# Layer 0's gated mixer: the gate product over all features for each chunk of K, with part of the conditioning on VectorE

## The chip, the cores and the metric

The kernel runs on one core of a Trainium2 chip. The core has five engines that work side by side, each through its own queue in order: TensorE (PE, with its weight loads shown as PEld), VectorE (DVE), ScalarE (ACT), GpSimd (POOL) and SyncE (SP), which here only issues transfers. Transfers run on 16 DMA engines. Matmuls write to PSUM, which has eight banks of 2 KB in each of 128 partitions. The metric is the device time of one execution in microseconds (us); several executions are timed and the median is given. One execution is also recorded by the hardware profiler; its times are counted from the start of the recorded span.

## The reference

A trunk of four layers over 256 tokens of width 1024, in float32. Each layer has a token mixer and a gated feed-forward part (FFN), and both are steered by a conditioning vector c. Layers 0 and 3 use a gated MLP as mixer. What matters here:

```python
c_act = jax.nn.silu(c)
mod = c_act @ ada_w[i] + ada_b[i]
sh1, sc1, g1, sh2, sc2, g2 = jnp.split(mod, 6, axis=-1)
h = modulate(rmsnorm(x, mix_norm_g[i]), sh1, sc1)
...
z = jax.nn.gelu(h @ w_in)
u, v = jnp.split(z, 2, axis=-1)
v = layernorm(v, ln_g, ln_b)
n = S // GM_CHUNK
v = v.reshape(B, n, GM_CHUNK, GM_GROUPS, GM_GROUP_DIM)
mask = jnp.tril(jnp.ones((GM_CHUNK, GM_CHUNK), dtype=bool))
ws = jnp.where(mask[None], w_s, jnp.zeros_like(w_s))
sv = jnp.einsum('gts,bnsgd->bntgd', ws, v) + b_s.T[None, None, :, :, None]
y = u * sv.reshape(B, S, GM_INNER)
return y @ w_out
```

`u` and `v` have 2048 features each. `mod` has 6 x 1024 values for each layer; the first 2048 (shift and scale) are needed before the first product of layer 0.

## The kernel before

The program is written with a framework that takes the instructions in program order, schedules them on the engines by priority and data, and sets the semaphores. The order in which the engines run them can therefore differ from the source; `tc.issue_after` forces an order on one engine.

**Products in three parts.** Weights come as 1 MB units of 128 x 2048 (`raw`, five buffers). `conv_half` splits a half unit into a rounded part `wh` (a cast on ACT, line 207) and the rest `wl` (a subtraction on VectorE, line 208), five buffers each. The activations are split in the same way into `hh` and `hlo`. `mm3` (lines 238 to 240) forms each product from three matmuls. `unit` hands out the next unit, and starts the loads and conversions of those after it.

**Conditioning.** `mod` of the layers is made in two ways. `ada_tensor` multiplies on TensorE (line 293). `ada_vector` multiplies rows of the weights with the spread vector `cbc` and sums them on VectorE (line 315), 1024 columns at a time, two for a 1 MB load. `pacing`, called once for each unit, starts such loads at the rates of `RATE` (a share of a load for each unit, for both kinds), and runs each two units later. In the last units of a stage it starts none (`left`). `need` runs what is still missing when its value is due.

**The first product.** For layer 0, `ada_first` (line 336) makes shift and scale for one chunk of 128 features at a time: a 1 MB load `adaf`, 64 small matmuls for each; `first_store` turns the result into columns (line 343), and `modulate_chunk` makes `nt`, `hh` and `hlo` of the chunk (lines 443 to 445). The order is written out by hand in `FIRST`: `a` is such a chunk of conditioning, `v` a chunk of the product, `d` the load of a unit, `p` the loads of late parameters and of the spread vector. The product `v` is computed token by feature, with K chunks of 128 inside. Its blocks 0 and 1 (1024 features, four banks) run along with the conditioning, chunk by chunk, from units that hold two K chunks each (`proj_tok_first`). Blocks 2 and 3 follow from units of 512 features (`proj_tok`).

**Behind it.** `gmlp` takes Gelu and sums of each block of `v` (line 561), squares around a provisional mean (line 575), the mean and root (lines 605 to 616). The layer-norm gain `Gb` and the bias `bs` come as one row and are spread by GpSimd (lines 584 and 592). `wsp`, the masked spatial weights times the inverse deviation, is made on VectorE (line 619), `v` is shifted and scaled in place (line 623), and `rsum`, the row sums of the spatial weights, come from TensorE (line 598). Then eight units of `u`: 48 products in `proj_pair`, four spatial matmuls `sv` (line 638), and the gating on VectorE and ACT (lines 632 to 646). The output product `go` (eight units) reads the gated `y` over 16 K chunks and updates `x`.

**PSUM.** The banks are four of tag `acc`, three of tag `misc` and one for `adaps`.

Of the kernel before, what the change touches and what calls it, by code (L numbers as in the profile page):

```python
# [8 lines left out]
F32 = mybir.dt.float32  # L9
# [29 lines left out]
FIRST = "a0 d v0 a1 a2 d v1 a3 v2 a4 d v3 a5 v4 a6 d v5 a7 v6 p v7"  # L39
# [10 lines left out]
RATE = {("mix", 0): (0.05, 0.4), ("u", 0): (0.1, 0.9), ("go", 0): (0.35, 0.7), ("up", 0): (0.05, 0.05),  # L50
# [41 lines left out]
def build(ctx, tc, A, out, stages=None):  # L92
# [34 lines left out]
    nc.scalar.dma_start(cin[:], A["c"])  # L127
    n0, n1 = _COLS["ada_b"] + 48, _COLS["lb"]
# [3 lines left out]
    ident = one.tile([P, P], F32, name="ident")  # L132
# [3 lines left out]
    def late_consts():  # L136
        with tc.issue_after(state["lastdma"]):
            nc.sync.dma_start(prm[:, n1:], A["prm"][:, n1:])
            nc.sync.dma_start(ident[:], A["ident"])
# [130 lines left out]
    adaps = pp.tile([P, 2, 256], F32, tag="ada", name="adaps", bufs=1)  # L270
# [6 lines left out]
    def ada_tensor(l, u):  # L277


        def load(i):  # L280
# [3 lines left out]
            def run():  # L284
                h = ADA_P.index((l, u)) % 2
                ps = adaps[:, h, :]
# [39 lines left out]
    def ada_first(l, c):  # L326

        raw = wp.tile([P, KC, 4, 64], F32, tag="raw", name=f"adaf{c}", bufs=NRAW)
        nc.sync.dma_start(raw[:].rearrange("p a b c -> p (a b c)"), A["ada0"][l, c])
        ps = misc(f"adaf{c}", (P, 64))  # L330
        with contextlib.ExitStack() as es:
            if "pe" in firsts:
                es.enter_context(tc.issue_after(firsts["pe"]))
            for kc in range(KC):
                for j in range(4):
                    i = pe.matmul(ps[32 * j : 32 * j + 32, :], crep(kc), raw[:, kc, j, :], start=kc == 0, stop=kc == KC - 1,
                                  tile_position=(0, 32 * j))
            firsts["pe"] = getattr(i, "ins", i)
        firsts[c] = ps

    def first_store(l, c):
        tr = t1(f"adaft{c}", 64)
        dve.transpose(tr[:], firsts[c][:])
        for e in range(2):
            b = 8 * e + c
            dve.tensor_tensor(mod[:, l, b : b + 1], tr[:, 32 * e : 32 * e + 1], prm[:, col("ada_b", l * 48 + b) : col("ada_b", l * 48 + b) + 1],
                              op=ALU.add)
        mod_post(l, 8 + c, 1)
# [158 lines left out]
    def proj_tok(blocks, name, sink, b0=0):  # L507

        for b in range(b0, blocks):
# [10 lines left out]
            for t in range(2):  # L520
                sink(b, t, ps[t])

    def proj_tok_first(name, sink, start=None):

        ps = [acc(f"{name}{i}") for i in range(4)]

        def chunk(kc):
            if kc % 2 == 0:
                firsts["w"] = unit(1, 0) if start else unit(2)
            with contextlib.ExitStack() as es:  # L530
                if start and kc < KC - 1:
                    es.enter_context(tc.issue_after(firsts["pe"]))
                for b in range(2):
                    a, bl = hl(firsts["w"], (kc % 2) * 1024 + b * 512, 512)
                    for t in range(2):
                        mm3(ps[2 * b + t][:], hh[:, kc, t * P : t * P + P], hlo[:, kc, t * P : t * P + P], a, bl, kc == 0, kc == KC - 1)
            firsts["pe"] = state["mm"]

        if start:
            start(chunk)  # L540
        else:
            for kc in range(KC):
                chunk(kc)
        for i in range(4):
            sink(i // 2, i % 2, ps[i])
# [10 lines left out]
    def gmlp(l, j, start=None):  # L556
        v = [big(f"v{t}") for t in range(2)]
        sums = sm("vsum", 8)

        def sink(b, t, ps):  # L560
            i = act.activation(v[t][:, 512 * b : 512 * b + 512], ps[:], AF.Gelu_apprx_tanh, accum_out=sums[:, 4 * t + b : 4 * t + b + 1])
            state["gelu"] = getattr(i, "ins", i)

        proj_tok_first("v", sink, start)
        if start:
            pace("mix", l, 20)
        proj_tok(3, "v", sink, 2)

        nsh = sm("nsh", 2)
# [8 lines left out]
        dve.tensor_reduce(nsh[:], sums[:].rearrange("p (t q) -> p t q", t=2)[:, :, 0:3], axis=AX.X, op=ALU.add)  # L578
        dve.tensor_scalar_mul(nsh[:], nsh[:], -4.0 / (3 * GI))
        for q in range(3):  # L580
            squares(q)
        Gb = big("Gb")
        nc.scalar.dma_start(Gb[0:1, :], A["gmg"][j : j + 1])
        pool.partition_broadcast(Gb[:], Gb[0:1, :])
        wr = big("ws", (P, 2, 8, P))
        ws = wr[:, 0]
        rsum = wr[:, 1]
        nc.scalar.dma_start(ws, A["gmws"][j])
        bs = big("bs", (P, 8, P))
        bsf = bs[:].rearrange("p g t -> p (g t)")  # L590
        nc.scalar.dma_start(bsf[0:1, :], A["gmbs"][j : j + 1])
        pool.partition_broadcast(bsf, bsf[0:1, :])
        proj_tok(4, "v", sink, 3)
        pool.affine_select(ws, ws, pattern=[[0, 8], [1, P]], compare_op=ALU.is_ge, fill=0.0, base=0,
                           channel_multiplier=-1)
        for h in range(2):
            ps = misc("rsum")
            pe.matmul(ps[:], onesw[:], wr[:, 0, 4 * h : 4 * h + 4, :].rearrange("p g t -> p (g t)"), start=True, stop=True)
            act.copy(rsum[:, 4 * h : 4 * h + 4, :].rearrange("p g t -> p (g t)"), ps[:])
# [17 lines left out]
        for g in (slice(0, 2), slice(2, 8)):  # L617
            for t in range(2):
                dve.tensor_scalar_mul(wsp[:, t, g], ws[:, g], rs[:, t : t + 1])
# [5 lines left out]
        pace("u", l)  # L625
        for i in range(8):
            ps = proj_pair(hk, lk, KC, f"u{i}")
            if i == 0:
                state["chain"] = tuple(getattr(s, "ins", s) for j, s in enumerate((warm, rec, root)) if GCH >> j & 1)
# [16 lines left out]
            split(yh(2 * i, 2), yl(2 * i, 2), u[:])  # L646
        pace("go", l)
# [248 lines left out]
    def hgrn(l):  # L896
# [51 lines left out]
        def isink(b, t, ps):  # L948
            act.copy(iv[:, t, 512 * b : 512 * b + 512], ps[:])
# [197 lines left out]
    if not quick:  # L1147
        nc.sync.dma_start(prm[:, n0:n1], A["prm"][:, n0:n1])
        nc.sync.dma_start(cbc[:], A["cb"])
        act.activation(cbc[:], cbc[:], AF.Silu)  # L1150
# [18 lines left out]
    for kind, l in stages:  # L1169
# [3 lines left out]
        if kind == "mix":  # L1173
# [3 lines left out]
            if l % 3 == 0:  # L1177
                if quick:
                    quick = False
                    ada_first(l, 0)  # L1180
                    bc0 = rms_bc(cur["st"], D, "n0")

                    def start(chunk):
                        for step in FIRST.split():
                            if step == "d":
                                dma_next()
                                continue
                            if step == "p":
                                with tc.issue_after(state["lastdma"]):
                                    nc.sync.dma_start(prm[:, n0:n1], A["prm"][:, n0:n1])  # L1190
                                conv_load(l)
                                late_c()
                                continue
                            c = int(step[1])
                            if step[0] == "a":
                                if c:
                                    ada_first(l, c)
                                first_store(l, c)
# [116 lines left out]
```

## Time and profile before

| | us |
|---|---|
| median of the three runs (1376.57 to 1381.03) | 1377.04 |
| the profiled execution | 1377.02 |
| its span | 1375.2 |
| start of the first v product, in the span | 11.84 |
| start of the first u product | 70.86 |
| end of the last u unit's sv, about | 124.4 |

The granted TensorE clock of the profiled execution is 0.998 of full speed. To read the tables: "busy" is the time in which an engine executes, and "idle before, releaser" the time in which it stood still ahead of an instruction, with the one that let it go. A row of the timeline has its start, its length, engine, source line, operation, output and inputs. Lengths of matmuls overlap, since they are pipelined: the distance of two starts is what one costs.

### The profile page before, as it was taken

How to read it: one execution, taken by the hardware profiler on the slowest of the kernel's cores; microseconds unless marked ns; L12 is line 12 of the kernel's file. 1: busy time of each engine (PE TensorE's matmuls, PEld its weight loads, DVE VectorE, ACT ScalarE, POOL GpSimd, SP SyncE). 2: the span in 40 equal slices, each digit the busy share in tenths (PEclk: the TensorE clock that was granted, in tenths of full speed). 3: DMA queues.
4: the chain of work that ended last, by engine and by line, in shares of the span. 5: the costliest groups of instructions: out<-in, count | busy, mean ns of one | idle time of the engine just before them, and what ended most of it. 6: DMA issues, size and time to landing. Idle time of an engine off the chain costs nothing.

```text
span 1375.2 us, 29290 instructions
## 1 busy us (share of the span) xinstructions
PE 1348.0 (98%) x12372; PEld 1283.2 (93%) x12372; DVE 1088.5 (79%) x1760; ACT 770.8 (56%) x1202; POOL 17.6 (1%) x19
## 2 busy tenths in 40 slices
PE   8999999999999999999999999999999999999997
PEld 6799999999998899999987889999987999999997
DVE  5699798889786798897789889889674863888843
ACT  3765366664466566654666546666356553666633
POOL 0100000000000000000010000000001000000000
PEclk9999999999999999999999999999999999999999
DMA  9869955557866366688576677558646464455531
GB/s 384 333 247 338 392 188 204 195 215 316 364 227 265 132 237 245 233 325 363 183 276 217 266 280 279 213 183 352 219 148 244 167 228 171 154 184 184 184 123 31
DMA packets 49483, 326.23 MB, mean 237 GB/s; under 512 B 5956, under 2 KB 9028, under 8 KB 11974
## 3 DMA queue, kind: packets, MB, share of 16 engines
q1 hardware_dynamic: 47568, 322.72, 62.2%
q8 instruction: 97, 1.59, 0.5%
q10 hardware_dynamic: 1784, 1.65, 0.3%
q14 instruction: 34, 0.28, 0.1%
HBM read 323.29 MB, written 1.05 MB: 236 GB/s over the span
## 4 chain that ended last, share of the span: by engine, by line
PE 92%; DMA 2%; DVE 2%; ACT 2%; issue 1%; DVEq 0%; SPq 0%; ACTq 0%
PE up L238 12%; PE up L239 12%; PE up L240 12%; PE dn L238 5%; PE dn L239 4%; PE dn L240 4%; PE go L238 2%; PE go L239 2%; PE go L240 2%; PE u L239 2%; PE u L238 2%; PE u L240 2%; PE adaps L293 2%; PE v L238 2%; PE v L239 2%; PE v L240 2%
## 5 line engine op out<-in xcount | busy, mean ns | idle before, releaser
L207 ACT CAST wh<-raw 128x1024 fp32r<-128x1024 f32 x426 | 434.8, 1031 | 387.8 <-PE up L239 170.0
L208 DVE TENSOR_TENSOR wl<-raw,wh 128x1024 fp32r<-128x1024 f32 x426 | 511.7, 1207 | 159.9 <-ACT wh L207 158.5
L238 PE MATMUL up<-hh,wh 128*128 128x256 f32 x1408 | 397.7, 283 | 2.6 <-ACT hh L444 2.5
L240 PE MATMUL up<-hh,wl 128*128 128x256 f32 x1408 | 397.6, 283 | 0.0
L239 PE MATMUL up<-hlo,wh 128*128 128x256 f32 x1408 | 397.4, 283 | 0.1
L238 PEld LDWEIGHTS up<-hh,wh 128*128 128x128 f32 x1408 | 269.7, 192 | 5.3 <-ACT hh L444 4.5
L239 PEld LDWEIGHTS up<-hlo,wh 128*128 128x128 f32 x1408 | 269.8, 192 | 0.6 <-DVE hlo L445 0.5
L240 PEld LDWEIGHTS up<-hh,wl 128*128 128x128 f32 x1408 | 270.1, 192 | 0.0
L238 PE MATMUL dn<-gh,wh 128*128 128x256 f32 x528 | 149.9, 284 | 1.5 <-ACT y L1094 1.5
L239 PE MATMUL dn<-gl,wh 128*128 128x256 f32 x528 | 149.4, 283 | 0.0
L240 PE MATMUL dn<-gh,wl 128*128 128x256 f32 x528 | 149.4, 283 | 0.0
L315 DVE CUSTOM_DVE_ANT_0 adaw<-adaw,cbc,prm 128x1024 f32<-128x1024 f32 x104 | 131.2, 1275 | 0.0
L1094 ACT ACTIVATE y<-up,cwb 128x256 f32<-128x256 f32 x176 | 98.6, 560 | 10.0 <-DVE y L1096 9.9
L238 PEld LDWEIGHTS dn<-gh,wh 128*128 128x128 f32 x528 | 101.3, 192 | 2.0 <-ACT y L1094 1.7
L239 PEld LDWEIGHTS dn<-gl,wh 128*128 128x128 f32 x528 | 101.3, 192 | 0.0
L240 PEld LDWEIGHTS dn<-gh,wl 128*128 128x128 f32 x528 | 101.3, 192 | 0.0
L1096 DVE SCALAR_TENSOR_TENSOR y<-up,cwb,y 128x254 f32<-128x254 f32 x176 | 84.5, 480 | 4.7
L1095 DVE SCALAR_TENSOR_TENSOR y<-up,cwb,y 128x255 f32<-128x255 f32 x176 | 83.9, 477 | 0.9 <-ACT y L1094 0.8
L238 PE MATMUL u<-hh,wh 128*128 128x256 f32 x256 | 74.0, 289 | 0.0
L238 PE MATMUL go<-yh,wh 128*128 128x256 f32 x256 | 73.3, 287 | 0.0
L240 PE MATMUL u<-hh,wl 128*128 128x256 f32 x256 | 72.4, 283 | 0.0
L239 PE MATMUL u<-hlo,wh 128*128 128x256 f32 x256 | 72.4, 283 | 0.0
(340 smaller groups left out, 2470.7 us busy)
## 6 DMA issues: line engine op xcount, KB each, us to landing
raw<-up SPq DMA_DIRECT2D x88, 1024.0 KB, 4.8
adaw<-adad SPq DMA_DIRECT2D x52, 1024.0 KB, 7.9
adaw<-adap SPq DMA_DIRECT2D x36, 1024.0 KB, 7.6
raw<-dn SPq DMA_DIRECT2D x32, 1024.0 KB, 4.8
raw<-gmu SPq DMA_DIRECT2D x16, 1024.0 KB, 4.8
raw<-gmo SPq DMA_DIRECT2D x16, 1024.0 KB, 4.8
raw<-gmv SPq DMA_DIRECT2D x15, 1024.0 KB, 6.2
raw<-dn SPq DMA_DIRECT2D x16, 768.0 KB, 5.4
```

Of the source, the lines that this page charges most:

```text
L207: act.copy(wh[:, :w], raw[:, o : o + w])
L208: i = dve.tensor_tensor(wl[:, :w], raw[:, o : o + w], wh[:, :w].bitcast(F32), op=ALU.subtract)
L238: pe.matmul(ps, lh, rh, start=start, stop=False)
L239: pe.matmul(ps, lh, rl, start=False, stop=False)
L240: i = pe.matmul(ps, ll, rh, start=False, stop=stop)
L293: pe.matmul(ps[32 * j : 32 * j + 32, :], crep(kc), raw[:, k, j, :], start=kc == 0, stop=kc == KC - 1, tile_position=(0, 32 * j))
L315: dve.tensor_tensor_reduce(raw[:, e, :], raw[:, e, :], cbc[:], 1.0, prm[:, c0 : c0 + 1], ALU.mult, ALU.add, mod[:, l, b : b + 1])
L1094: act.activation(y[:], ps[:, e, :], AF.Identity, bias=b, scale=w[2])
L1095: dve.scalar_tensor_tensor(y[:, 1:], ps[:, e, : S - 1], w[1], y[:, 1:], op0=ALU.mult, op1=ALU.add)
L1096: dve.scalar_tensor_tensor(y[:, 2:], ps[:, e, : S - 2], w[0], y[:, 2:], op0=ALU.mult, op1=ALU.add)
```

## The change

- `v` of layer 0 is computed over all 2048 features for each K chunk, in eight PSUM banks (four `acc`, three `misc`, and the one of `ada`, which is now allocated when it is first used). The units of `gmv` for layer 0 hold one K chunk each.
- The conditioning of chunks 0 and 1 (`FIRSTPE = 2`) stays on TensorE; that of chunks 2 to 7 is computed on VectorE, from weights laid out for it.
- `cbc` is no longer loaded: TensorE spreads the vector with an identity matrix (`spread`), which is loaded early on ACT's queue; two VectorE copies take it from PSUM.
- The broadcast of the norm is copied to SBUF (`bcs`), so that its bank is free.
- `ws`, `Gb` and `bs` are loaded from SP in the last chunk of `v`, the latter two replicated by the transfer; GpSimd's two broadcasts go.
- `wsp` is made on ACT, and in layer 0 the copies of `rsum` on VectorE.
- The gating of a unit of `u` comes two units later (in layer 0), and catches up in the last two.
- The rates of `u` and `go` in layer 0 change, and the rate of the mixer's start isn't used any more.

```diff
-FIRST = "a0 d v0 a1 a2 d v1 a3 v2 a4 d v3 a5 v4 a6 d v5 a7 v6 p v7"
+FIRSTPE = 2
...
-RATE = {("mix", 0): (0.05, 0.4), ("u", 0): (0.1, 0.9), ("go", 0): (0.35, 0.7), ("up", 0): (0.05, 0.05),
+RATE = {("mix", 0): (0.05, 0.4), ("u", 0): (0.1, 0.75), ("go", 0): (0.35, 0.9), ("up", 0): (0.05, 0.05),
...
+    ident = one.tile([P, P], F32, name="ident")
+    nc.scalar.dma_start(ident[:], A["ident"])
...
-    def late_c():
-        with tc.issue_after(state["lastdma"]):
-            nc.sync.dma_start(cbc[:], A["cb"])
-        act.activation(cbc[:], cbc[:], AF.Silu)
+    def spread():
+
+        for h in range(2):
+            ps = misc(f"cbc{h}")
+            for k in range(4):
+                kc = 4 * h + k
+                pe.matmul(ps[:, k * P : k * P + P], cact[:, kc : kc + 1].broadcast_to([P, P]), ident[:], start=True, stop=True)
+            dve.tensor_copy(cbc[:, 512 * h : 512 * h + 512], ps[:])
...
+    def first_load(l, c):
+
+        raw = wp.tile([P, 2048], F32, tag="raw", name=f"adaf{c}", bufs=NRAW)
+        nc.sync.dma_start(raw[:], A["ada0"][l, c])
+        firsts[c] = raw
+
+    def first_run(l, c):
+        raw = firsts.pop(c)
+        if c >= FIRSTPE:
+
+            v = raw[:].rearrange("p (e k) -> p e k", e=2)
+            for e in range(2):
+                b = 8 * e + c
+                c0 = col("ada_b", l * 48 + b)
+                dve.tensor_tensor_reduce(v[:, e], v[:, e], cbc[:], 1.0, prm[:, c0 : c0 + 1], ALU.mult, ALU.add, mod[:, l, b : b + 1])
+        else:
...
+    def proj_tok_all(l, name, bc0, bc):
+
+        make = [acc] * 4 + [misc] * 3 + [ada]
+        ps = {}
+
+        def products(kc, w, blocks):
...
+                for b in blocks:
+                    a, bl = hl(w, b * 512, 512)
                     for t in range(2):
+                        if kc == 0:
+                            ps[b, t] = make[2 * b + t](f"{name}{b}{t}", (P, 512))
+                        mm3(ps[b, t][:], hh[:, kc, t * P : t * P + P], hlo[:, kc, t * P : t * P + P], a, bl, kc == 0, kc == KC - 1)
             firsts["pe"] = state["mm"]
 
...
+        modulate_chunk(l, 0, 0, bc0)
+        dma_next()
+        first_load(l, 1)
+        dma_next()
+        first_load(l, 2)
+        for kc in range(KC):
+            w = unit(2) if kc == KC - 1 else unit(1, 0)
+            if kc + 1 < FIRSTPE:
+
+                products(kc, w, (0, 1))
+                first_run(l, kc + 1)
+                products(kc, w, (2,))
+                modulate_chunk(l, 0, kc + 1, bc)
+                products(kc, w, (3,))
+            else:
+                products(kc, w, range(4))
+                if kc < KC - 1:
+                    first_run(l, kc + 1)
+                    modulate_chunk(l, 0, kc + 1, bc)
+            if kc + 2 < KC:
+                dma_next()
+            if kc + 3 < KC:
+                first_load(l, kc + 3)
+            if kc == KC - 3:
+                with tc.issue_after(state["lastdma"]):
+                    nc.sync.dma_start(prm[:, n0:n1], A["prm"][:, n0:n1])
+                conv_load(l)
+            if kc == KC - 1:
+                lnp["now"] = ln_load(l // 3)
+        return ps
...
+    def ln_load(j):
+
+        Gb = big("Gb")
+        wr = big("ws", (P, 2, 8, P))
+        bs = big("bs", (P, 8, P))
+        with tc.issue_after(state["lastdma"]):
+            nc.sync.dma_start(wr[:, 0], A["gmws"][j])
+            nc.sync.dma_start(Gb[:], A["gmg"][j : j + 1].broadcast_to([P, GI]))
+            nc.sync.dma_start(bs[:].rearrange("p g t -> p (g t)"), A["gmbs"][j : j + 1].broadcast_to([P, 8 * P]))
+        return Gb, wr, bs
...
         if start:
-            pace("mix", l, 20)
-        proj_tok(3, "v", sink, 2)
...
+            ps = proj_tok_all(l, "v", *start)
+            for b in range(4):
+                if b == 3:
+                    shift()
+                for t in range(2):
+                    sink(b, t, ps[b, t][:])
+
+            conv_half()
+            conv_half()
...
-            act.copy(rsum[:, 4 * h : 4 * h + 4, :].rearrange("p g t -> p (g t)"), ps[:])
+            (dve.tensor_copy if start else act.copy)(rsum[:, 4 * h : 4 * h + 4, :].rearrange("p g t -> p (g t)"), ps[:])
+        if start:
+            conv_half()
...
-                dve.tensor_scalar_mul(wsp[:, t, g], ws[:, g], rs[:, t : t + 1])
+                act.activation(wsp[:, t, g], ws[:, g], AF.Copy, scale=rs[:, t : t + 1])
...
+        pace("u", l, *((16,) if start else ()))
+        us = []
+        for i in range(8):
+            ps = proj_pair(hk, lk, KC, f"u{i}")
+            if i == 0:
+                state["chain"] = tuple(getattr(s, "ins", s) for j, s in enumerate((warm, rec, root)) if GCH >> j & 1)
+            us.append((i, ps))
+            while len(us) > (min(2, 7 - i) if start else 0):
+                gating(*us.pop(0))
...
+    spread()
     act.activation(sm("warm", 1)[:], sq0[:, SQACT[-1], 0:1], AF.Sqrt)
...
-                    ada_first(l, 0)
+                    first_load(l, 0)
+                    first_run(l, 0)
                     bc0 = rms_bc(cur["st"], D, "n0")
...
+                    bcs = big("bcs", (P, S))
+                    act.copy(bcs[:], bc0[:])
+                    gmlp(l, l // 3, (bc0[:], bcs[:]))
...
-    r["gmv"] = np.stack([np.concatenate([atk(w[:, GI : GI + D]), at(w[:, GI + D :])]) for w in wi])
+
+    r["gmv"] = np.stack([wi[0][:, GI:].reshape(8, P, 2048), np.concatenate([atk(wi[1][:, GI : GI + D]), at(wi[1][:, GI + D :])])])
```

`gating(i, ps)` is the old body of the loop over `u`, unchanged, from the Gelu to the split of `y`.

More of the change, by code (lines that the diff above doesn't have):

```diff
@@ L324, in build @@
     firsts = {}
[L326 to L339, printed above, removed]
@@ L576, in squares @@
                                accum_out=ss[:, 4 * t + q : 4 * t + q + 1])
-        dve.tensor_reduce(nsh[:], sums[:].rearrange("p (t q) -> p t q", t=2)[:, :, 0:3], axis=AX.X, op=ALU.add)
-        dve.tensor_scalar_mul(nsh[:], nsh[:], -4.0 / (3 * GI))
         for q in range(3):
             squares(q)
[L582 to L585, printed above, removed]
+        Gb, wr, bs = lnp.pop("now") if start else ln_load(j)
         ws = wr[:, 0]
         rsum = wr[:, 1]
[L588 to L593, printed above, removed]
+        if not start:
+            proj_tok(4, "v", sink, 3)
         pool.affine_select(ws, ws, pattern=[[0, 8], [1, P]], compare_op=ALU.is_ge, fill=0.0, base=0,
@@ L624, in gmlp, with gating @@
         yh, yl = hilo("y", 16)
[L625 to L629, printed above, removed]
+        def gating(i, ps):
             u = t2("u", (P, 2, S))
```

100 lines of the change are left out of this document (46 added, 54 removed).

## The prediction

> **What bounds the kernel now.** I read the page first, for the engine that fills the span.
>
> ```profile
> span 1375.2 us, 29290 instructions
> PE 1348.0 (98%) x12372; PEld 1283.2 (93%) x12372; DVE 1088.5 (79%) x1760; ACT 770.8 (56%) x1202; POOL 17.6 (1%) x19
> PE 92%; DMA 2%; DVE 2%; ACT 2%; issue 1%; DVEq 0%; SPq 0%; ACTq 0%
> ```
>
> TensorE bounds nearly everything. The chain of waits gives DMA only 2%, and the change touches layer 0's mixer alone, so the question is how much TensorE time lies at its front. The windows view splits that mixer at the first u product and the first go products; its columns are busy time of PE, PEld, DVE, ACT and POOL, granted clock, DMA share and GB/s. The last row is a window of its own.
>
> ```profile
> 0.00:70.86 70.86, 63.32 (x804) 50.74 (x805) 43.02 (x82) 40.38 (x65) 6.08 (x9) 1.00 0.91 360
> 70.86:127.00 56.14, 56.14 (x473) 56.03 (x472) 56.03 (x96) 31.33 (x44) 0.00 (x0) 1.00 0.76 283
> 127.00:173.00 46.00, 46.00 (x428) 44.77 (x427) 35.42 (x49) 17.73 (x23) 0.00 (x0) 1.00 0.95 368
> 10.00:35.00 25.00, 21.12 (x407) 16.53 (x410) 16.19 (x42) 8.91 (x12) 0.00 (x0) 1.00 1.02 421
> ```
>
> From 70.86 us on TensorE never rests, and VectorE is as full as TensorE until 127. Ahead of it the DMA engines are saturated: 421 GB/s from 10 to 35 us. The chain of waits, in order of time (start, length, what), has a transfer as its longest piece there:
>
> ```profile
> 24.44 10.65 DMA raw<-gmv
> ```
>
> The timeline of TensorE (start, length, instruction, idle time before it) gives the ends of this stretch and its prices:
>
> ```profile
> 11.84 0.96 PE L238 MATMUL v<-wh,hh 128*128 128x512 f32 x3 [1.11 <-ACT hh L444]
> ...
> 17.74 1.10 PE L336 MATMUL adaf<-adaf,cact 128*32 128x64 f32 x64 [1.39 <-DMA adaf<-ada]
> 18.77 0.50 PE L238 MATMUL v<-wh,hh 128*128 128x512 f32 x1
> ...
> 58.17 0.39 PE L238 MATMUL v<-wh,hh 128*128 128x512 f32 x1
> ...
> 62.70 0.39 PE L240 MATMUL v<-wh,hlo 128*128 128x512 f32 x1
> 62.93 1.88 PE L598 MATMUL rsum<-ws,ones 128*128 128x512 f32 x4
> 64.48 0.79 PE L238 MATMUL v<-wh,hh 128*128 128x512 f32 x2
> ...
> 70.86 0.28 PE L238 MATMUL u<-hh,wh 128*128 128x256 f32 x1
> ```
>
> The first v product starts at 11.84 and u at 70.86: 59.0 us. The starts 58.17 and 62.70 are 20 products apart, 0.227 us each, so the 192 v products (4 blocks x 8 chunks x 2 halves x 3) need 43.6. A conditioning group of 64 small matmuls holds TensorE for 1.03 (17.74 to 18.77); seven lie in the stretch: 7.2. The row sums (rsum) take 1.55 (62.93 to 64.48). That leaves about 6.7 us without work. The reason is the order of loads: while 9 MB of x and conditioning weights arrive, only half of the v products are allowed, those of blocks 0 and 1.
>
> **The change, part by part.** *All 2048 features per chunk.* Each 1 MB unit now feeds 24 products, 5.45 us, beside 2 MB of loads per chunk. Three floors for the start of u follow.
>
> TensorE: 11.84 + 43.6 + one conditioning group 1.0 = 56.4.
>
> DMA: the fifth megabyte (with x) landed at 17.74. The last v unit is the 17th; twelve more at 1.049 MB / 421 GB/s = 2.49 us bring it at 47.6. Cast and subtraction of its first half and the last 22 products put u at about 55.
>
> VectorE: six of the eight conditioning groups move to it. Its prices, in the timeline:
>
> ```profile
> 58.96 1.27 DVE L315 CUSTOM_DVE_ANT_0 adaw<-adaw,cbc,prm 128x1024 f32<-128x1024 f32 x1
> 60.16 1.27 DVE L315 CUSTOM_DVE_ANT_0 adaw<-adaw,cbc,prm 128x1024 f32<-128x1024 f32 x1
> 64.46 4.63 DVE L208 TENSOR_TENSOR wl<-raw,wh 128x1024 fp32r<-128x1024 f32 x4 [3.02 <-ACT wh L207]
> 176.70 0.87 DVE L443 SCALAR_TENSOR_TENSOR nt<-x,amul,bcn 128x256 f32<-128x256 f32 x2
> 177.49 1.30 DVE L445 SCALAR_TENSOR_TENSOR hlo<-nt,mod,hh 128x256 fp32r<-128x256 f32 x3
> 47.27 2.95 ACT L207 CAST wh<-raw 128x1024 fp32r<-128x1024 f32 x3
> ```
>
> Back to back a reduction of 1024 columns costs 1.20, a subtraction (wl) 1.16, nt and hlo 0.43 each. A chunk is two reductions, two subtractions, nt, hlo and the small amul (0.1): 5.7 us, more than TensorE's 5.45 or DMA's 4.98. So **VectorE sets the pace**, narrowly. Unit 1 is now the fifth megabyte, 17.7; cast 0.98 and two subtractions end at 21.0. Six rounds (chunks 2 to 7) of 5.7 end at 55.2. In the last one hlo and the first half's subtraction are done about 54.1, one subtraction earlier; 22 products remain from there: u at 59.1. I add 0.6 for hand-overs between engines and 0.5 for the start, below: **60.2**.
>
> *Vector spread by PE.* Its eight matmuls of 128 columns are not in the trace; the sv rows are the nearest, four matmuls as eight passes in 0.89.
>
> ```profile
> 8.59 1.10 PE L336 MATMUL adaf<-adaf,cact 128*32 128x64 f32 x64 [1.09 <-DMA adaf<-ada]
> sel<-sel ACTq DMA_DIRECT2D x1, 2.0 KB, 7.0
> 90.28 0.89 PE sv L638 x8
> 96.92 0.89 PE sv L638 x8
> ```
>
> That makes 1.8 us in TensorE's queue ahead of the statistics; 1.09 hides in the wait for the first conditioning weights. The identity (64 KB, 0.16 us of DMA) goes ahead of sel on ACT's queue, and the broadcast waits for sel. Bounds 0 and 2 us; I take 0.5, since the next deadline, unit 1 at 17.7, is a DMA's. The two copies to cbc fall into VectorE's idle time about there. The replicated vector (0.5 MB) and its Silu go; they cost nothing on the path.
>
> *Layer-norm loads ahead, no POOL.* rsum moves behind v: 1.55 of the gain goes back. The replicated Gb and bs and ws are 2 MB on SP's queue, behind unit 9 and ahead of unit 10 (u2's weights): some 5 us at 421 GB/s, while u0 and u1 have theirs. A load whose source row is read by all 128 partitions is not in the trace, so this price has a rival below. Dropping the broadcasts on POOL is worth something to VectorE:
>
> ```profile
> 51.08 2.95 POOL L584 PARTITION_BROADCAST Gb<-Gb  x1 [50.04 <-DMA Gb<-gmg]
> L208 DVE TENSOR_TENSOR wl<-raw,wh x11: 1214/1219/3180, 43.7 to 69.3; 128x1024 fp32r<-128x1024 f32 x11
> ```
>
> One subtraction took 3.18 instead of 1.22 us in the time of a broadcast. That did not hold TensorE, so I count nothing.
>
> *Gating two units behind, wsp on ACT.* All Gelus of v now come at its end, and the chain behind them is long. The view by lines has its prices (busy us, mean ns, idle before):
>
> ```profile
> L575 ACT ACTIVATE jk<-v,nsh 128x512 f32<-128x512 f32 x8 | 5.7, 714 | 0.8 <-DVE nsh L579 0.8
> L561 ACT ACTIVATE v<-v 128x512 f32<-128x512 f32 x8 | 4.7, 595 | 5.1 <-PE v L240 5.1
> L609 ACT ACT_TABLE_LOAD x1 | 1.3, 1283 | 0.0
> L619 DVE TENSOR_SCALAR wsp<-ws,vrs 128x768 f32<-128x768 f32 x2 | 1.1, 617 | 0.0
> L645 DVE TENSOR_TENSOR u<-u,gt 128x512 f32<-128x512 f32 x8 | 5.4, 678 | 0.0
> ```
>
> The Gelus (0.6 each) keep up with a bank's six products per pair, so the last ends 1 us after v. Then come the squares 5.7, up to four weight casts 4.0, a table load 1.3, the small VectorE steps and the root about 1.3: 13.3 us. wsp on ACT is not shown; from below VectorE's 1.1 for the two large ones, from above four full casts, 3.9; I take 2.4 (it writes as many columns as two casts), in all 15.7. Queued behind the root on ACT are wsp, the first u Gelu and unit 11's cast. The first sv needs wsp behind rsum and three u units; sv follows sv by 6.65 (90.28 to 96.92), so a unit is 5.76 and sv comes at 1.55 + 17.3 = 18.8 us. It is covered with 3 us over; without the lag this would be a stall of 8 us. At the end the lag is paid: sv6 and sv7 come together, and y of both needs six VectorE steps like L645, 4.1 us, beside go's first subtractions; go0 has 36 products (0.12 each, 5.76 / 48) before it needs the earlier of the two, 4.3 us. I take 0.6, between 0 and 2.
>
> *Rates.* The first vector load starts later, and eleven instead of twelve are planned by the end of go; the twelfth is forced by the FFN's modulation.
>
> ```profile
> 160.01 0.43 SPq L309 DMA_DIRECT2D adaw<-adad  x1
> 172.25 0.48 DVE L459 SCALAR_TENSOR_TENSOR x<-go,gate,x 128x256 f32<-128x256 f32 x1 [4.58 <-PE go L240]
> ```
>
> Before, SP issued the thirteenth, which belongs behind the modulation, at 160.0, and VectorE then idles 4.58 us before 172.25: room for two reductions. I count nothing; without that cover it costs a megabyte's 2.5 and two reductions, 5 in all.
>
> **Sum.** u starts 70.86 - 60.2 = 10.7 us earlier; less 1.55 (rsum) and 0.6 (end of gating): 8.5. Everything later is TensorE bound and shifts along. The profiled execution took 1377.02 (span 1375.2 and 1.8 around it), the median shown is 1377.04; the forecast is 1377.0 - 8.5 = **1368.5 us**.
>
> **Rivals.** *VectorE is not the bound* (wl, nt and hlo slip into each other's waits, or TensorE lags anyway). Then u starts at TensorE's floor, 56.4 to 57: 12 us gained, 1365. For it: the three floors are within 4 us. Against: VectorE has the longest round.
>
> *Waits inside the VectorE round.* hlo waits for ACT's hh, and a poor order pays it each chunk:
>
> ```profile
> 42.76 0.48 DVE L445 SCALAR_TENSOR_TENSOR hlo<-nt,mod,hh 128x256 fp32r<-128x256 f32 x1 [0.58 <-ACT hh L444]
> ```
>
> Six times 0.58 is 3.5; with a loose end of gating 1.5 more: 3.5 gained, 1373.5. Against: before already puts a subtraction between nt and hlo elsewhere.
>
> *The replicated loads are slow, and it ends slower.* Behind them on SP stands unit 10. They are issued about 50.5 (unit 9 needs unit 6's buffer, free a round before 55.2, and the start's slip counts); at full rate unit 10 lands near 61, after 4 MB, and is needed near 69, its cast and subtraction before u2's 71.7, so 8 us are spare. The two loads' 1.57 MB may then take 3.8 + 8 = 12 us (131 GB/s) for nothing; each further us delays u2 by one. At 20.5 us (77 GB/s) the gain is gone, at 27.5 (57 GB/s) the kernel takes 1384. For it: no load here reads one row 128 times. Against: the same 16 engines ran at 421 GB/s on rows of equal length.
>
> [...]
>
> *It buys nothing*: the normalization chain outlasts its cover, or the forced twelfth load comes late; 5 us of either, with 2 us more of loose ends, leave 1.5, 1375.5. Against: 3 us over, and the issue row.
>
> **Chances.** Forecast (6.5 to 10.5 gained) 0.50, floor of TensorE 0.15, waits in the round 0.18, nothing bought 0.10, slow loads 0.07. A measurement of this kernel can tell about 0.3%, 4.1 us, from no change. Faster takes the first two whole and most of the third: 0.80; slower half of the slow loads and a tail of the fourth: 0.06; the rest is same: 0.14. The range reaches from 1364, just beyond TensorE's floor, to the fourth case's 1375.5.
>
> **What would show it.** In the changed profile: the first u product near 60 (56 to 57 says TensorE bound, 63 or more says waits); 12 reductions of 1.27 us before it and VectorE without idle time from 21 to 55; hlo without a wait for hh; rsum behind v; the first sv without an idle TensorE ahead of it; Gb landing within 10 us. A gap on TensorE before u2 or the first sv, or a first go product that waits for y, would make the prediction wrong; so would a loss at the FFN's start.

## The result, and the profile after

The changed kernel takes 1387.51 us (median of four runs, 1386.16 to 1388.24), beside 1377.2 for the kernel before in the same comparison: a ratio of 1.0063, 95% interval 1.0048 to 1.0078. It is slower by about 9 us by the ratio, 10.3 by the medians, where 8.5 less was forecast. The profiled execution took 1388.24, its span 1386.5, at a granted clock of 0.992. First the page of the changed kernel: span, engines, and the chain of waits by engine.

```profile
span 1386.5 us, 28569 instructions
PE 1353.7 (98%) x12004; PEld 1286.2 (93%) x12004; DVE 1100.3 (79%) x1762; ACT 771.5 (56%) x1207; POOL 8.0 (1%) x15
PE 89%; DVE 7%; ACT 3%; issue 1%; DVEq 0%; POOL 0%; ACTq 0%; POOLq 0%
```

VectorE's share of the chain rose from 2% to 7%, TensorE's fell from 92% to 89%, and the page doesn't say where. For that I cut both spans at the first TensorE product of each stage and set the lengths side by side. The columns for two experiments are used below.

| stage (us) | before | after | a_count | a_pace |
|---|---|---|---|---|
| to the first v | 11.84 | 13.69 | 13.9 | 14.3 |
| layer 0 v | 59.02 | 50.64 | 49.53 | 49.36 |
| layer 0 u | 53.30 | 56.09 | 56.09 | 56.09 |
| layer 0 go | 53.16 | 55.24 | 55.22 | 54.00 |
| layer 0 FFN, up | 128.34 | 129.82 | 129.82 | 128.27 |
| layer 0 FFN, down | 69.52 | 69.52 | 69.52 | 69.52 |
| layer 1 mixer | 88.26 | 90.49 | 88.25 | 88.24 |
| layer 1 FFN, up | 128.27 | 132.52 | 129.53 | 129.75 |
| layer 1 FFN, down | 71.50 | 74.38 | 71.51 | 71.51 |
| layer 2 mixer | 158.18 | 160.20 | 159.24 | 159.72 |
| layer 2 FFN and layer 3 mixer | 352.5 | 351.4 | 352.6 | 352.6 |
| layer 3 FFN, to the end | 201.3 | 202.5 | 203.2 | 201.4 |

The same in rows of the windows view (busy time of PE, PEld, DVE, ACT, POOL, granted clock, DMA share, GB/s), first of the changed kernel: the start, then the three stages of layer 1 (mixer, up, down).

```profile
0.00:64.33 64.33, 59.78 (x432) 48.05 (x432) 51.18 (x83) 29.62 (x40) 2.34 (x7) 0.95 0.97 376
...
375.00:465.49 90.49, 88.58 (x804) 77.48 (x804) 69.38 (x155) 53.30 (x117) 0.61 (x2) 1.00 0.62 233
465.49:598.02 132.53, 129.61 (x1077) 127.61 (x1073) 113.90 (x187) 79.99 (x128) 0.00 (x0) 1.00 0.62 226
598.02:672.39 74.37, 71.95 (x664) 69.14 (x664) 59.35 (x93) 33.37 (x49) 2.28 (x2) 0.98 0.81 308
```

And of the kernel before, the same three stages of layer 1:

```profile
375.18:463.43 88.25, 86.11 (x788) 77.08 (x788) 67.15 (x153) 53.37 (x117) 0.61 (x2) 1.00 0.53 204
463.43:591.70 128.27, 128.25 (x1072) 127.33 (x1073) 116.00 (x193) 79.34 (x128) 0.00 (x0) 1.00 0.66 242
591.70:663.20 71.50, 70.64 (x666) 67.41 (x665) 57.10 (x89) 34.18 (x49) 0.00 (x0) 1.00 0.77 304
```

Two things are to be seen. In layer 0, u starts 6.5 us earlier (64.33 for 70.86), and by the end of the first up stage the kernel has only 0.17 of it left (305.49 for 305.66): u, go and up gave it back. And layers 1 and 2, whose code the diff doesn't touch, lost 11.4: in the layer-1 up stage TensorE idles 2.9 us of 132.53, where it idled 0.02 before.

**What changed in layer 1.** At the start of its down stage VectorE is late. The timeline of VectorE in the changed kernel, then that of TensorE:

```profile
603.91 0.48 DVE L1178 SCALAR_TENSOR_TENSOR y<-up,cwb,y 128x255 f32<-128x255 f32 x1
604.31 1.28 DVE L325 CUSTOM_DVE_ANT_0 adaw<-adaw,cbc,prm 128x1024 f32<-128x1024 f32 x1
...
605.51 0.48 DVE L1179 SCALAR_TENSOR_TENSOR y<-up,cwb,y 128x254 f32<-128x254 f32 x1
```

```profile
606.14 0.36 PE L243 MATMUL dn<-gh,wh 128*128 128x256 f32 x1 [2.15 <-DVE y L1179]
```

A reduction of the conditioning (L325) stands between the two VectorE steps of a convolution (y, L1178 and L1179) that the down product waits for, and TensorE stands still for 2.15 us. This one reduction accounts for 1.2 of them (604.31 to 605.51). The kernel before has one between the same two steps as well, and its TensorE doesn't wait there:

```profile
594.00 0.48 DVE L1095 SCALAR_TENSOR_TENSOR y<-up,cwb,y 128x255 f32<-128x255 f32 x1
594.39 1.28 DVE L315 CUSTOM_DVE_ANT_0 adaw<-adaw,cbc,prm 128x1024 f32<-128x1024 f32 x1
...
595.60 0.48 DVE L1096 SCALAR_TENSOR_TENSOR y<-up,cwb,y 128x254 f32<-128x254 f32 x1
```

The likely difference is how many come together: around the start of the down stage the changed kernel begins four reductions within 8.1 us (596.2 to 604.3), the kernel before three (589.4 to 597.5). That was not tested by itself; the experiments below show that the stage follows the counters. The 2.15 also lie ahead of a half-clock stretch (a granted clock of 0.50 from 606.82 to 610.23); the last section is about these.

The view of waits of the changed kernel has six more waits for y, in the up stage (us in total, times, longest), where the kernel before has none:

```profile
PE up L243 <- DVE y L1179: 2.4, 6, 0.4
```

They come from 558.6 to 590.5, 6.4 us apart, and no reduction runs on VectorE meanwhile: the last starts at 549.2, the next at 596.2. The chain of waits ahead of the first of them, whose product starts at 558.58, is a cast, a subtraction and the two steps of y:

```profile
555.21 1.06 ACT wh L212
556.29 1.23 DVE wl L213
557.52 0.41 DVE y L1178
557.95 0.49 DVE y L1179
```

The cast in turn waits for a TensorE product, so this is a loop, and it recurs for each of the six. The products behind these waits start 0.68 us after the one before, instead of 0.12: together 3.4 of the 4.3 us that the stage lost. What starts the loop was not tested by itself; ahead of it stand four reductions (538.0 to 549.2) where the kernel before has two (536.0 and 539.1).

The reductions are placed by `pacing`. It keeps two counters, one for loads that TensorE works off and one for loads that VectorE works off; each unit adds the rate of its stage, at one a load starts, and **the remainder is carried into the next stage and the next layer**. Followed through the source, the FFN of layer 0 was entered with 0.35 and 0.9999999 before, and with 0.15 and 0.4 after. At 0.05 a unit, the next vector load then starts some 12 units later. The traces bear that out: two reductions in the first up stage instead of four, one more in the down stage and one more in the layer-1 mixer, which also has the 16 further TensorE rows of the windows view (804 for 788).

### The profile page after: what moved, and what is told of

Read it like the earlier page. It is cut to its first block, busy times and chain, and to the rows that moved or that the text cites. A ratio compares the mean times of both kernels' runs of the same rounds, so it can differ in the third digit from the quotient of the medians.

```text
span 1386.5 us, 28569 instructions
## 1 busy us (share of the span) xinstructions
PE 1353.7 (98%) x12004; PEld 1286.2 (93%) x12004; DVE 1100.3 (79%) x1762; ACT 771.5 (56%) x1207; POOL 8.0 (1%) x15
## 3 DMA queue, kind: packets, MB, share of 16 engines
q8 instruction: 94, 1.54, 0.4%
## 4 chain that ended last, share of the span: by engine, by line
PE 89%; DVE 7%; ACT 3%; issue 1%; DVEq 0%; POOL 0%; ACTq 0%; POOLq 0%
PE up L243 12%; PE up L244 12%; PE up L245 12%; PE dn L243 5%; PE dn L245 4%; PE dn L244 4%; DVE wl L213 2%; PE go L243 2%; PE adaps L303 2%; PE go L244 2%; PE go L245 2%; PE u L243 2%; PE u L244 2%; PE u L245 2%; ACT wh L212 1%; PE v L243 1%
## 5 line engine op out<-in xcount | busy, mean ns | idle before, releaser
L325 DVE CUSTOM_DVE_ANT_0 adaw<-adaw,cbc,prm 128x1024 f32<-128x1024 f32 x104 | 131.7, 1275 | 3.0 <-DMA adaw<-adad 3.0
L1177 ACT ACTIVATE y<-up,cwb 128x256 f32<-128x256 f32 x176 | 98.7, 561 | 11.2 <-DVE y L1179 10.6
L1179 DVE SCALAR_TENSOR_TENSOR y<-up,cwb,y 128x254 f32<-128x254 f32 x176 | 84.6, 481 | 5.0
L1178 DVE SCALAR_TENSOR_TENSOR y<-up,cwb,y 128x255 f32<-128x255 f32 x176 | 83.9, 477 | 0.7 <-ACT y L1177 0.6
L244 PE MATMUL go<-yl,wh 128*128 128x256 f32 x256 | 72.5, 283 | 0.3 <-DVE yl L484 0.3
```

Of the source, the lines that this page charges most:

```text
L244: pe.matmul(ps, lh, rl, start=False, stop=False)
L325: dve.tensor_tensor_reduce(raw[:, e, :], raw[:, e, :], cbc[:], 1.0, prm[:, c0 : c0 + 1], ALU.mult, ALU.add, mod[:, l, b : b + 1])
L1177: act.activation(y[:], ps[:, e, :], AF.Identity, bias=b, scale=w[2])
L1178: dve.scalar_tensor_tensor(y[:, 1:], ps[:, e, : S - 1], w[1], y[:, 1:], op0=ALU.mult, op1=ALU.add)
L1179: dve.scalar_tensor_tensor(y[:, 2:], ps[:, e, : S - 2], w[0], y[:, 2:], op0=ALU.mult, op1=ALU.add)
```

## The experiments

"Before" is timed beside each; ratios are to it.

**1. Counters restored, and go's rate raised (a_pace).**

```diff
-RATE = {... ("go", 0): (0.35, 0.9), ...
+RATE = {... ("go", 0): (0.35, 1.0), ...
...
+            if l == 0:
+                state["p"], state["d"] = 0.35, 0.9999999
```

The two lines stand ahead of layer 0's FFN.

> The changed kernel, with the counters of the conditioning loads as they stood before: a go rate of 1.0 (twelve vector loads by the end of go instead of eleven), and the fractions 0.35 and 0.9999999 put back ahead of layer 0's up product. Between the start of that product and the end the changed kernel lost 13.0 us against the one before (up starts 1.7 us earlier, the end comes 11.3 us later). Theory 'pacing': those 13 us come from where the shifted counters put the conditioning work in layers 1 and 2. Then most of it comes back: 1374 to 1379 us, and the stages from layer 1's mixer to layer 2's mixer are within 2 us of before. Rival 'front': the later loss follows from what layer 0's mixer leaves behind (late loads, the clock). Then the time stays above 1384.

Measured: 1374.94 us, ratio 0.9978 (0.9968 to 0.9987). From the first up stage on, each stage is as long as in the kernel before, to 0.1 us, but for the layer-1 up stage (+1.5), where the granted clock is 0.50 from 461.24 to 464.65, discussed below, and the layer-2 mixer (+1.5); what lengthened that one was not shown. With the counters as they were and go's rate raised, the change is worth 0.2%, 3.0 us by the ratio.

**2. The same in the kernel before: its counters set to the changed kernel's (b_pace).**

```diff
+            if l == 0:
+                state["p"], state["d"] = 0.15, 0.4
```

> The kernel before, with the counters that the changed kernel has ahead of layer 0's up product (0.15 and 0.4), and nothing else of the change. TensorE's instructions from there on stand in the same order as in the changed kernel. Theory 'pacing': 11 to 13 us slower than before, 1387 to 1390, with the loss in layer 1's mixer, up and dn and in layer 2's mixer, as in the changed kernel. Rival 'front': within 2 us of before, 1375 to 1379.

Measured: 1389.19, ratio 1.0077 (1.0061 to 1.0092), 10.6 us more without any change to layer 0's mixer. The windows view of this run has the changed kernel's layer-1 mixer and up stage almost to the hundredth (the down stage is 74.39, at a granted clock of 0.98 in both), with the same six waits for y:

```profile
375.35:465.83 90.48, 88.58 (x805) 77.47 (x805) 69.35 (x155) 53.21 (x117) 0.61 (x2) 1.00 0.62 233
465.83:598.31 132.48, 129.57 (x1077) 127.57 (x1073) 113.87 (x187) 79.91 (x128) 0.00 (x0) 1.00 0.62 226
```

**3 and 4. One counter at a time in the kernel before (b_p: only 0.15; b_d: only 0.4).**

> The kernel before, with the counter of the TensorE kind of conditioning loads alone set to 0.15 ahead of layer 0's up product (b_pace with one of its two settings). Theory 'vector counter': the slower stretches come from vector loads that fall one unit later, so this one stays within 2 us of 1377.2, and b_d has the 10 us. Rival 'TensorE counter': eight instead of seven groups in layer 1's mixer (2.2 us there) and what follows it: 1385 or more. Third: every other setting loses against the one that the rates were set for, and both lose: each 1380 or more.

> The kernel before, with the counter of the vector kind alone set to 0.4 there. Theory 'vector counter': 1385 to 1389. Rival 'TensorE counter': within 2 us of 1377.2. Third, as with b_p: each of the two 1380 or more.

Measured: b_p 1379.77, ratio 1.0008 (0.9996 to 1.0020); b_d 1385.68, ratio 1.0048 (1.0029 to 1.0067). The vector counter carries most of it: b_d alone has the layer-1 up stage at 132.86. The TensorE counter adds 1.5 to the layer-1 mixer and little to the time. By the ratios the two alone come to 7.7 us, both together to 10.6; the rest was not traced.

**5. Only the counters, go's rate as the change has it (a_count).** The two lines of a_pace without its new rate.

> The changed kernel with the two counters of pacing set to 0.35 and 0.9999999 at the start of layer 0's FFN, and the rates of layer 0 left as the change has them (go 0.9). Theory 'the counters alone carry the loss': the end of go stays as in the changed kernel (go about 55.2, the forced twelfth load; the first FFN stage 128.3 or 129.8 with a half-clock stretch), and every stage from layer 0's down product on is as long as in a_pace; 1 to 3 us above a_pace's 1374.9, so 1376 to 1378, and 9 to 11 below the changed kernel's 1387.5. Rival 'the go rate did it, the counters little': 1384 or more.

Measured: 1378.63, ratio 0.9998 (0.9988 to 1.0008). So the counters are worth 8.9 of the changed kernel's 1387.51, a little less than forecast (the run is 0.6 above the range given), and without them the change as it stands is worth nothing. The mixer and the down stage of layer 1 are back at the lengths of before (the table). In its up stage, by the windows view, TensorE no longer idles (129.51 busy of 129.53); what is left there is 1.3, at a granted clock of 0.99 where before had 1.00:

```profile
462.33:591.86 129.53, 129.51 (x1072) 128.79 (x1073) 116.00 (x193) 79.37 (x128) 0.00 (x0) 0.99 0.66 239
```

The step from a_count to a_pace is go's rate: 3.7 us by the medians, 2.8 by the ratios. The reason stands at the end of go, in the timeline of the changed kernel:

```profile
169.29 0.48 DVE L479 SCALAR_TENSOR_TENSOR x<-go,gate,x 128x256 f32<-128x256 f32 x1 [3.37 <-PE go L245]
169.69 1.27 DVE L325 CUSTOM_DVE_ANT_0 adaw<-adaw,cbc,prm 128x1024 f32<-128x1024 f32 x1
...
170.89 0.42 DVE L445 TENSOR_TENSOR sq<-x 128x256 f32<-128x256 f32 x1
```

The last reduction of the forced twelfth load stands between the update of x and the square that the next norm needs (sq), though VectorE had idled 3.37 us just before. With go's rate at 1.0 the load is planned, sq follows x at once, and go is 1.2 shorter; the half-clock stretch that followed (0.50 from 176.74 to 180.15) is gone too, 1.5 more: the first up stage has a clock of 0.99 in the changed kernel and 1.00 in a_pace.

**6. The spread moved behind the first statistics (a_spread_late).**

```diff
-    spread()
...
+                    spread()
```

> The changed kernel, with the matmuls that spread the vector behind the norm's broadcast instead of ahead of the statistics. Theory 'start': the spread delays the first product (13.69 instead of 11.84 us), and TensorE's idle time of 1.92 us ahead of it lets the granted clock fall to 0.5 from 12.9 to 19.7; in the new place the spread fills that hole. Then no half clock in the first 20 us, v starts by 12.5, u 3 to 4 us earlier than 64.3, and the time is about 1384. Rival 'VectorE': the pace of the rounds is all that counts, u starts at 63.5 or later, and the time stays within 1 us of 1387.5.

Measured: 1389.35, ratio 1.0078 (1.0059 to 1.0098); 1384 was expected. The broadcast of the norm needs sel, and sel had not landed:

```profile
10.93 1.94 PE L435 MATMUL bcn<-rsn,sel 128*128 128x64 f32 x8 [2.90 <-DMA sel<-sel]
```

TensorE idled 2.90 where the spread had been, and the first v product came at 17.3 instead of 13.69.

**7. No lag of the gating (a_lag0).**

```diff
-            while len(us) > (min(2, 7 - i) if start else 0):
+            while len(us) > 0:
```

> The changed kernel with the gating right behind each u unit again. Theory of the prediction: the normalization chain takes about 15 us behind v, so TensorE waits some 8 us ahead of the first sv: 1393 to 1396. Rival 'order': the scheduler puts the next unit's products ahead of sv by itself, as it did before, and the time stays within 2 us of 1387.5.

Measured: 1386.96, ratio 1.0059 (1.0040 to 1.0078), no different from the changed kernel. The timeline of TensorE of this run:

```profile
79.16 2.05 PE L711 MATMUL sv<-wsp,v 128*128 128x128 f32 x16 [0.80 <-ACT wsp L696]
```

u starts at 63.3 and wsp comes at 79.16, 15.9 later, which is the length forecast for the normalization chain. But TensorE loses 0.80 for it, not 8: the framework runs the products of the next unit ahead by itself, and the spatial matmuls of the first two units come together (x16). Over u and go the kernel with and without lag are equally long (+4.85 and +4.87 against before).

**8. An earlier start (a_start).** On top of a_pace: sel is loaded ahead of the parameters on ACT's queue, the identity behind them, and the spread stands behind the broadcast of the norm.

> The kernel of the run a_pace (the change with the counters of before), with sel ahead of the parameters and the identity last on ACT's queue, and the spread behind the norm's broadcast on TensorE. In the run a_spread_late the broadcast waited 2.90 us for sel, and the clock fell there. Theory 'start': with sel early, the broadcast is done by 10.9, v starts by 13, the clock does not fall before 20 us, u starts 2.5 to 3.5 us earlier than in a_pace (63.7), and the time is 1371 to 1373. Rival 'VectorE': rounds that start earlier only wait for the loads; u within 1 us of 63.7 and the time within 1 us of a_pace's 1374.9.

Measured: 1375.56, ratio 0.9976 (0.9966 to 0.9986). v starts at 13.2 and u at 62.48, 1.2 earlier than in a_pace, half of what was expected, and the time isn't the 1371 to 1373 expected. The profiled span is 1.6 shorter than a_pace's (1373.1 for 1374.7, at a granted clock of 0.996 for 0.994), the median isn't; that difference is about as large as the 1.5 by which the up stages with a half-clock stretch came out longer (last section).

**9. Lighter reductions (a_halfred).** On top of a_pace, the reductions of chunks 2 to 7 run over 512 of 1024 columns: half of the sum over K is left out of that conditioning.

```diff
-                dve.tensor_tensor_reduce(v[:, e], v[:, e], cbc[:], ...
+                dve.tensor_tensor_reduce(v[:, e, :512], v[:, e, :512], cbc[:, :512], ...
```

> The kernel of the run a_pace, with the reductions of chunks 2 to 7 over 512 instead of 1024 columns: half of the K sum of the conditioning of these chunks is left out. VectorE's round falls by some 1.2 us, below TensorE's. Theory 'VectorE sets the pace': the rounds fall from 5.87 to TensorE's 5.46, and u starts 2.5 us earlier than in a_pace (61.2), the time near 1372.5. Rival 'another bound' (loads, buffers, or ACT's casts hold the round): u within 0.7 us of 63.7.

Measured: 1376.31, ratio 0.9981 (0.9971 to 0.9991), u at 63.46. The reductions fall from 1.20 to 0.67 each and the rounds don't get shorter: 5.94, where the theory had 5.46, and u is within the rival's 0.7. Its chain of waits, in order of time, gives the reason:

```profile
30.95 0.50 DVE nt L463
...
31.47 0.04 ACT hh L464
...
31.89 1.04 ACT wh L212
...
32.95 2.36 DVE wl L213 x2
35.32 0.66 DVE adaf L350
```

A ring runs through ACT: the reductions give nt, ACT makes hh of it and only then casts the next weights (wh), VectorE subtracts (wl), and only then come the next reductions. It is as long as VectorE's own work.

**10 and 11. The casts asked for one chunk ahead, on top of a_start (a_ahead) and of a_halfred (a_half_ahead,** with the same half of the sum left out**).**

```diff
-            w = unit(2) if kc == KC - 1 else unit(1, 0)
+            w = unit(2) if kc == KC - 1 else unit(2 if kc else 1, 0)
```

> a_start with each chunk's casts and subtractions asked for one chunk ahead, reductions over all 1024 columns. Theory 'ring through ACT, and VectorE's own work just as long': taking the ring away leaves VectorE's own round of 5.7 to 5.9 us, so u starts within 0.7 us of a_start's 62.5 and the time is within 1 us of 1375.6. Rival 'the ring alone sets the round': rounds fall to TensorE's 5.45 us, u about 2 us earlier, 60.5.

> a_halfred (reductions over 512 of 1024 columns, so half of the sum over K of the conditioning of chunks 2 to 7 is left out) with casts and subtractions asked for one chunk ahead. Theory 'ring through ACT': with VectorE some 1.2 us a round lighter and the ring opened, rounds fall from a_halfred's 5.94 to TensorE's 5.45 or so, and u starts about 2.5 us earlier than a_halfred's 63.5, near 61; time about 1374. Rival 'yet another bound, loads or TensorE's own order': rounds stay at 5.9 and u within 0.7 us of 63.5.

Measured: a_ahead 1376.49, ratio 0.9987 (0.9977 to 0.9997); a_half_ahead 1376.50, ratio 0.9986 (0.9977 to 0.9995). In a_ahead the subtractions no longer wait behind nt, and the chain of waits has VectorE alone, at 5.79 a round (its reductions start at 35.63 and 41.42). So VectorE's own work does bound the rounds with full reductions. Its u comes at 64.3 all the same, outside the 0.7 expected: v starts 1.4 later than in a_start, behind small matmuls of the conditioning (adaf) that take 1.86 in its chain of waits, for 1.07 in a_start's, and the last hlo holds TensorE for 0.76. In a_half_ahead the edit didn't open the ring: ACT still ran hh ahead of both casts, the rounds stayed at 5.94 and u at 63.48, and what lies under both rings wasn't seen.

**12. Unit 9's casts behind the Gelus of v (a_gelu),** on top of a_start:

```diff
+            state["chain"] = (state["gelu"],)
             conv_half()
             conv_half()
```

> a_start with one order forced: unit 9's two weight casts stand behind the last Gelu of v on ACT, where a_start has them between the Gelus. Theory 'casts hold up u': the first u product and the row sums each wait about 0.95 us for the last Gelus of v, and those are late because the casts stand ahead of them. Then u starts about 1 us earlier than a_start's 62.5, the u stage is again about 1 us shorter, and the time falls by 1.5 to 2 us to about 1373.8. Rival 'the casts come late in their turn': u starts earlier, but the first u products wait for unit 9's weights; the sum of both stages and the time stay within 0.7 us of a_start's 1375.6.

Measured: **1373.60, ratio 0.9966 (0.9953 to 0.9978), the lowest median of all**, though the interval overlaps those of a_start and a_pace. In the changed kernel the first u product and the row sums wait for Gelus on ACT (timeline of TensorE):

```profile
64.33 0.39 PE L243 MATMUL u<-hh,wh 128*128 128x256 f32 x1 [0.52 <-ACT v L637]
...
66.74 1.96 PE L673 MATMUL rsum<-ws,ones 128*128 128x512 f32 x4 [0.94 <-ACT v L637]
```

and in a_gelu neither does:

```profile
63.08 0.28 PE L243 MATMUL u<-hh,wh 128*128 128x256 f32 x1
...
64.27 1.93 PE L674 MATMUL rsum<-ws,ones 128*128 128x512 f32 x4
```

The u stage is 54.85, which is before's 53.30 and the 1.55 of rsum, nothing else. u itself came at 63.08 rather than 61.5, as v started at 14.6, behind a spread that takes 3.26 in its chain of waits, for 2.05 in a_start's timeline; the median fell by the 2.0 expected (1.4 by the ratios).

## Why the prediction was wrong, step by step

**The step that failed first** is the sentence "Everything later is TensorE bound and shifts along", with the paragraph on rates before it, which follows the loads to the end of go and stops there. The stages behind are TensorE bound only while VectorE's reductions fall where nothing waits for them, and the remainder of the counters decides where they fall. Forward (b_pace) that remainder cost 10.6 us, backward (a_count) 8.9. By the ratios that is about 9 of the 17 us between forecast and result; the rest is the sum for layer 0, which failed too, and is taken apart next. No rival had the counters, so the range couldn't hold the time; the rival on the other side was another mechanism, and it wasn't this one.

**The sum for layer 0**: 8.5 forecast, 0.2 in the trace (6.5 at u's start, less 2.8 in u, 2.1 in go, 1.5 in up), and by a_count nothing in the time. Term by term:

- *Start of u, 60.2, was 64.33.* VectorE's pace was right: the chain of waits of the changed kernel has it back to back, 5.87 a round for the 5.7 forecast, 1.0 over six rounds. The start was mis-sized:

```profile
6.38 2.02 PE cbc L165 x16
...
24.53 1.19 DVE adaf L350
...
30.40 1.20 DVE adaf L350
```

  The rounds begin at 24.53, not 21.0. I held the next deadline to be a transfer's and took 0.5 of a bound of 2. The spread takes 2.02 ahead of the statistics, the first v product comes 1.9 later than before, and then there is a price that no row of before had: a granted clock of 0.50 from 12.9 to 19.7. The windows view of the changed kernel:

```profile
13.00:20.00 7.00, 6.31 (x56) 4.69 (x60) 1.71 (x3) 1.68 (x3) 0.00 (x0) 0.52 1.01 420
```

  The last half microsecond is the wait for the Gelu shown above: I had them keep up with the banks, but on ACT the casts of the next unit stood ahead of them, and a table load of 1.28 (at 62.30). Together 3.5, 1.0 and 0.5, less the 1.1 that the sum had added for hand-overs and the start, are 3.9 of the 4.1.
- *rsum, 1.55:* right in size; it brought a wait of 0.94 for ACT's last Gelus, which a_gelu took away.
- *The lag:* the length of the chain was right (15.7 and 15.9), and so was that it is covered (the first sv at 84.59 waits for nothing), but "without the lag this would be a stall of 8 us" was wrong by ten times: 0.80.
- *The end of the gating, 0.6,* was about right: in a_pace, without the forced load, go is 0.8 longer than before (54.00 for 53.16).
- *The forced twelfth load, "I count nothing"*, with 5 named as its price without cover: it cost 2.8 by the ratios of a_count and a_pace. The idle time of VectorE was there, but the reduction wasn't run in it; it came behind x, where the square waits for it. This is the loss at the FFN's start that the prediction named as a sign of being wrong.
- *The rivals:* VectorE was the bound (a_ahead), not TensorE; "waits inside the round" is half there, since the ring through ACT is as long. The replicated loads were not slow. The view of the DMA issues of the changed kernel (KB each, us to landing):

```profile
Gb<-gmg SPq DMA_DIRECT2D x1, 1024.0 KB, 8.3
```

  That time holds the queueing too, among loads that come to 386 GB/s in all (40 to 60 us), and no u product waited for it.

## What to carry to other kernels

Where work is spread over a program by running counters, a change of one stage moves everything behind it: compare the order of instructions behind the change before believing that the rest "shifts along", and pin the counters when only the front is to be judged. A forced piece of work isn't run in the idle time that the old trace shows, but where the scheduler finds it due: look at what is next on that engine. And what one gains at the start of a pipelined stretch is worth what the next engine in order leaves of it: here casts ahead of Gelus on ACT, and a reduction ahead of a square on VectorE, cost some 2.0 and 2.8 us of the 8.5 forecast.

## What was not expected of the hardware

**A stretch at half clock follows a wait of 1.54 us in one run and not in another.** Before, TensorE waits 1.54 ahead of the layer-1 up stage and the granted clock stays at 1.00. The timeline and the windows view of before:

```profile
463.43 0.62 PE L238 MATMUL up<-hh,wh 128*128 128x256 f32 x3 [1.54 <-ACT hh L444]
```

```profile
461.49:464.90 3.41, 1.85 (x16) 1.25 (x11) 2.95 (x9) 1.73 (x4) 0.00 (x0) 1.00 0.01 2
464.90:468.31 3.41, 3.41 (x31) 3.41 (x30) 3.41 (x9) 2.02 (x5) 0.00 (x0) 1.00 0.00 0
```

In a_pace a stretch at half clock comes behind the same wait:

```profile
459.77 0.62 PE L243 MATMUL up<-hh,wh 128*128 128x256 f32 x3 [1.54 <-ACT hh L464]
```

```profile
457.83:461.24 3.41, 1.85 (x16) 1.25 (x11) 2.95 (x9) 1.73 (x4) 0.00 (x0) 1.00 0.00 0
461.24:464.65 3.41, 3.41 (x19) 3.41 (x18) 3.41 (x9) 2.02 (x5) 0.00 (x0) 0.50 0.02 5
```

The upper rows agree in all busy times and instruction counts, 1.85 us of TensorE among them, and the lower ones have a clock of 1.00 before and 0.50 in a_pace. In the changed kernel such stretches begin at 176.74, 606.82 and 1183.67, each 3.41 long at 0.50, and the one at 12.9 lasted twice as long, 6.8. In the 3.41 us ahead of these four TensorE was busy for 1.85, 1.26, 1.52 and 1.91. Two up stages with one came out 1.5 longer than before (129.82 for 128.34 in layer 0 of the changed kernel, 129.75 for 128.27 in layer 1 of a_pace). Nor does one follow every such idle time: in the changed kernel TensorE waits 2.01 ahead of 748.71 and is busy for only 1.47 between 746.77 and 750.18, and the clock is 1.00 from 746 to 755. So these runs don't show that TensorE's idle time by itself lets the clock fall, as the theory of a_spread_late has it; what decides it they don't settle, nor why the stretch at 12.9 was the longer one. Some of the experiments' misses of 1 to 2 us may hang on it (a_start, a_ahead, a_count), so the small terms are known no better than that.
